# A convolution pair of the in-projection moved from plain column tiles to seven-product form, with the scan and token work around it

## The chip, the cores and the metric

The kernel runs on one core of a Trainium2 chip. The metric is the device time of one execution in microseconds, and the number compared is the median of several executions. Beside it there is one profiled execution, from which all rows of the trace are taken.

## What is computed

The reference is one layer of a decoder trunk on x of 1024 positions by 1024 channels, in float32:

```python
h = rms_norm(x, g_mix[l])
z = jnp.einsum("bsd,de->bse", h, w_in[l]) + b_in[l]
va, ga, xb, gb, sa, sb = jnp.split(z, cuts, axis=-1)      # 1024, 1024, 1536, 1536, 1024, 1024 columns

u = va * jax.nn.sigmoid(ga)
u = causal_depthwise_conv(u, conv_a_w[l], conv_a_b[l])    # width 31
u = jax.nn.silu(layer_norm(u, ln_g[l], ln_b[l]))
y_a = jnp.einsum("bsc,cd->bsd", u, w_a_out[l])

v = causal_depthwise_conv(xb, conv_b_w[l], conv_b_b[l])   # width 4
v = rg_lru(v, w_rg_a[l], b_rg_a[l], w_rg_x[l], b_rg_x[l], lam[l])   # 16 heads of 96, a scan along the positions
y_b = jnp.einsum("bsc,cd->bsd", v * jax.nn.gelu(gb), w_b_out[l])

m = jax.nn.sigmoid(sa) * y_a + jax.nn.sigmoid(sb) * y_b
x = x + jnp.einsum("bsd,de->bse", m, w_o[l])
h = rms_norm(x, g_mlp[l])
f = jnp.square(jax.nn.relu(jnp.einsum("bsd,df->bsf", h, w_1[l])))
x = x + jnp.einsum("bsf,fd->bsd", f, w_2[l])
return rms_norm(x, g_final)
```

The change concerns the first two lines with z, the product that makes u, and the recurrence.

## The kernel before

**Precision.** Every operand of a large product is split into a high and a low part (float32r), and a product takes three passes: high by high, high by low, low by high. The low part of a weight is made in one of two ways. Either ScalarE writes the high part and VectorE subtracts, or, in `split_dma` (line 63), ScalarE writes the negated source into the low tile, an accumulating DMA of the GpSimd queue adds the source to it (line 66), and ScalarE writes the high part.

**The in-projection in two parts.** The 56 column tiles of 128 columns (VA and GA: convolution branch and its gate, 8 each; XB and GB: recurrence and its gate, 12 each; SA and SB: the two output gates, 8 each) are computed in two stages.

The first part (line 827) has one slot for each entry of the list CH, numbered s, up to NC1 - 1. A slot's product is `chunk_mm` (line 734): 24 steps by two halves of the positions, 48 matmuls. Between its two halves and behind them stand the products of the 16 recurrence heads (`head_mm`, line 544, six matmuls for each gate), about one head for a slot from slot 4 on, head 15 at slot 21 with its second product in slot 22. They write a PSUM tile of which there is one buffer ("ps2"), which ScalarE's sigmoid (`head_gate`, line 555) empties. A column tile of XB goes through a convolution of width 4 (`xb_out`); a pair VA, GA makes u (`u_gate`, a sigmoid on ScalarE, line 603; `u_mul` on VectorE, line 609).

The second part (line 1038) takes pairs of column tiles, listed in ZPAIRS, and computes each pair as a two by two block product with seven block products instead of eight (`z_mm`, line 936: 12 matmuls for each, so 84 for a pair). It needs sums and differences of blocks of the weights (`z_sums`, line 766), prepared weights for each product (`z_lhs`, line 781), and differences of blocks of the tokens: `x_load` (line 680, four transfers from the DRAM copy xu into four tiles), `x_sum` (line 686, four subtractions on VectorE), `x_parts` (line 691, splits into high and low). Products 1, 2 and 3 use the token tiles that the first part has; 6, 7, 5 and 4 need the new ones, in this order of first use. The order of the products of all pairs is written out in `zseq` (line 797): (0,1), (1,1), (0,2), (1,2), (0,6), (0,7), (1,7), (0,5), and so on, as (pair, product). At the step n, `z_mm` is issued for zseq[n] and `z_lhs` for zseq[n + 4]; the weights of the first two, (0,1) and (1,1), are prepared in the last slot of the first part (lines 898 to 900), those of the next two just behind it.

**The recurrence.** Tiles come in four groups of three. For the last group (tiles 9 to 11) `scan_exp` (line 569: for each tile an exponential and a tanh on ScalarE) stands in slot 22, `scan_root` (line 580: three square roots) in slot 23, and `scan_tile` (line 591: product, product, scan, and the store to hd, on VectorE and SyncE) in slots 23, 24 and 25. Those of the group before are in slots 20, 21 and 22. Each of the gates of head 15 is brought to its tiles by three transfers on SyncE's queue (line 565).

**The convolution of width 31.** Each of the 8 tiles of u takes 49 VectorE operations (`conv`, line 620). They are the filler: `fill` (line 459) puts them where its plan of VectorE's time has room.

**What sets the order.** ScalarE, VectorE, TensorE, SyncE and GpSimd issue in the order in which the code is written, in this stage on all five. Work for VectorE that is handed to `later` (line 713) is sorted by its due time at the end of each slot or step (`vector_work`, line 717); the order of the others is that of the calls. What is done in which slot around the border stands in two tables: XS (line 818, by slot of the first part) and ZX (line 1036, by step of the second).

**Buffers.** Most tiles of 128 by 1024 come from one pool, tag "T", with 37 buffers (line 36). An instruction that makes a new tile waits on its own queue until a buffer has been given back by the last user of an earlier tile. In use through the border are 14 token tiles (xh, xl), the running sum of the convolutions, gates, decays and v of the scans, u with two working tiles for the convolution under way, and the token differences. The weights of the second part come into another four buffers, tag "p" (`z_load`, line 753), which heads 3, 7, 11 and 15 use as well, two each (line 524).

Of the kernel before, what the change touches and what calls it, by code (L numbers as in the profile page):

```python
# [30 lines left out]
def trunk_kernel(ctx: ExitStack, tc: tile.TileContext, x, xt_in, xt_eo, vecs, w_in, w_a_out, w_b_pl, w_b_sq,  # L31
# [413 lines left out]
    VA, GA, XB, GB, SA, SB = 0, 8, 16, 28, 40, 48  # L445
# [121 lines left out]
    at_, rooted = {}, {}  # L567
# [23 lines left out]
    def scan_tile(t):  # L591
# [4 lines left out]
        nc.vector.tensor_tensor_scan(i, a, i, 0.0, ALU.mult, ALU.add)  # L596
        nc.sync.dma_start(hd[t], i)

    ut = {}
    yd = dp.tile([8, P, S], F32, name="yd")  # L600
    ysum = []
# [100 lines left out]
                      ALU.subtract)  # L702

    CH = [XB, VA, GA, XB + 1, XB + 2, VA + 1, GA + 1, XB + 3, XB + 4, XB + 5, VA + 2, GA + 2]
    CH += [XB + t for t in range(6, 12)] + [c for j in range(3, 7) for c in (VA + j, GA + j)]
    NU = 7
    CH[-2:] = CH[:-3:-1]
    NC1 = len(CH)
    zps = {n: z0[n] for n in range(N0)}
# [3 lines left out]
    def later(ready, cost, f, *a):  # L713

        todo.append((ready, len(todo), cost, f, a))
# [28 lines left out]
                                 start=n == 0, stop=n == 23)  # L744
        at("P", len(halves) * (n1 - n0) * MM)

    ZPAIRS = [GB + 2 * i for i in range(6)] + [VA + 7] + [SA + 2 * i for i in range(4)]
    ZPAIRS += [SB + 2 * i for i in range(4)]
    NZ = len(ZPAIRS)
    zraw, zs, zo, zb = {}, {}, {}, {}  # L750
    zn = [0]

    def z_load(i, kk):

        zraw[i, kk] = raw = qp.tile([P, 2, 4, P], F32, tag="p", name=f"zw{i}_{kk}", bufs=4)
        c = ZPAIRS[i]
        if c < GA:
# [51 lines left out]
    def z_get(n, f):  # L809
# [5 lines left out]
    head_at = {s: n for n, s in enumerate(HS0)}  # L815

    EXP = {head_slot: g for g, head_slot in enumerate(HS0[4 * g + 3] + 1 for g in range(4))}
    XS = {NC1 - 5: ((x_load, 0),), NC1 - 4: ((x_sum, 0),), NC1 - 3: ((x_load, 1), (x_parts, 0, 6)),
          NC1 - 2: ((x_sum, 1), (x_parts, 0, 7, 5)), NC1 - 1: ((x_parts, 0, 4), (x_parts, 1, 6))}
    made = []  # L820
    head_w(0)
    w_load(3)
# [4 lines left out]
    with tc.manual_schedule(engines=ENGINES):  # L827
        for s in range(3, NC1):
# [30 lines left out]
            c = CH[s - 1]  # L859
# [27 lines left out]
            for d in range(5):  # L887
                if s - d in EXP:
# [6 lines left out]
                    t = 3 * g + d - (2 if g < 3 else 1)  # L895
                    if 3 * g <= t < 3 * g + 3:
                        later(rooted[t], 4.8, scan_tile, t)
            if s == NC1 - 1:
                z_get(0, z_lhs)
                z_get(1, z_lhs)  # L900
            for f, *a in XS.get(s, ()):
                f(*a)
# [71 lines left out]
    def z_out(i, m_, hf, src, name):  # L974
        if ZPAIRS[i] < GA:
            z_u(i, ZPAIRS[i] - VA, m_, hf, src)
            return
        ci = ZPAIRS[i] + m_
        bias = bin_c[:, ci:ci + 1]
# [53 lines left out]
        elif p == 4:  # L1033
            z_out(i, 1, 0, zb[i, "u"], "c")

    ZX = {0: ((x_parts, 1, 7),), 2: ((x_parts, 1, 5),), 4: ((x_parts, 1, 4),)}
    H_AT = {2: (0, 0), 5: (1, 1), 3: (0, 1), 4: (1, 0)}
    with tc.manual_schedule(engines=ENGINES):

# [154 lines left out]
        z_get(3, z_lhs)  # L1194
        u_mul(NU - 1, zps[NC1 - 1])
        vector_work(clk["V"])
        z_h(0, 0, 0)
        for n in range(len(zseq) + 2):
# [9 lines left out]
            if n + 3 < len(zseq):  # L1208
                i, p = zseq[n + 3]
# [760 lines left out]
    with tc.manual_schedule(engines={mybir.EngineType.Activation, mybir.EngineType.DVE,  # L1970
                                     mybir.EngineType.PE}):
        for n in range(len(useq)):
# [4 lines left out]
            while ready < min(len(useq), n + look + 1):  # L1977
                i, p = useq[ready]
# [316 lines left out]
```

## Time and profile before

| | |
|---|---|
| median of 3 runs | 1529.34 us (1529.16 to 1529.37) |
| the profiled execution | 1528.49 us, its span 1526.7 us |
| mean granted clock of TensorE | 0.999 |
| first matmul of the first part's slots in the list above (line 743) | 42.4 us |
| first matmul of the second part (line 944) | 338.56 us |
| last convolution operation (line 662) | 583.59 us |

The page gives busy times of the engines, the busy share in 40 slices, the DMA queues, the chain of work that ended last, and the costliest groups. A timeline row has the start, the time, the engine, the line, the operation, output<-input, and in brackets the idle time before it with what ended it. PE is TensorE, DVE is VectorE, ACT is ScalarE, POOL is GpSimd's queue, SP is SyncE's, and SPq is its issuing of a DMA. A window row has, for PE, PEld, DVE, ACT and POOL, the busy time in the stretch, then the granted clock, the DMA share and GB/s.

### The profile page before, as it was taken

To read this page: it belongs to the slowest core of one execution; us is meant where nothing else is said; L and a number is where in the kernel's file an instruction comes from. 1 tells how busy PE (TensorE), PEld (TensorE's weight loads), DVE (VectorE), ACT (ScalarE), POOL (GpSimd) and SP (SyncE) were. 2 spreads that over 40 slices of the span, in tenths; PEclk is the share of its full clock that TensorE was granted. 3 is DMA by queue.
4 is the path that set the end of the run, shared out by engine and by line. 5 is a ranking of instruction groups with operands and counts; after the bars stand their busy time and mean duration, and the time that the engine had idled before them with its cause. 6 is when DMAs were issued, how large, how long until landed. Compare 5 with 4: busy or idle time off the path is not lost.

```text
span 1526.7 us, 18955 instructions
## 1 busy us (share of the span) xinstructions
PE 1517.1 (99%) x6712; PEld 1248.3 (82%) x6712; DVE 1200.7 (79%) x1640; ACT 928.1 (61%) x1299; POOL 190.7 (12%) x228
## 2 busy tenths in 40 slices
PE   9999999999999999999999999999999999999998
PEld 7878887888888888888888888888888888888886
DVE  6999996999999997788769879755555387777777
ACT  6748688576566667645475777554444455545475
POOL 0111011022222222000022322000000000101010
PEclk9999999999999999999999999999999999999999
DMA  8757778698997789964779897333333974776464
GB/s 352 192 135 165 178 179 187 199 262 211 266 254 179 182 207 277 304 216 120 268 197 302 191 213 174 124 127 111 111 111 111 308 264 125 181 206 171 106 124 152
DMA packets 130911, 295.48 MB, mean 194 GB/s; under 512 B 12800, under 2 KB 34944, under 8 KB 130816
## 3 DMA queue, kind: packets, MB, share of 16 engines
q1 hardware_dynamic: 98960, 214.83, 41.5%
q0 software_dynamic: 31568, 78.92, 27.4%
q8 instruction: 52, 0.85, 0.2%
q10 hardware_dynamic: 288, 0.52, 0.1%
q14 instruction: 43, 0.35, 0.1%
HBM read 148.74 MB, written 60.82 MB: 137 GB/s over the span
## 4 chain that ended last, share of the span: by engine, by line
PE 99%; DMA 0%; DVE 0%; ACT 0%; SPq 0%; issue 0%
PE z L743 16%; PE d2b L2015 2%; PE d1b L2015 2%; PE d0b L2015 2%; PE z L273 2%; PE d3b L2015 2%; PE d0e L2015 1%; PE d3e L2015 1%; PE d3a L2015 1%; PE d2e L2015 1%; PE d1e L2015 1%; PE d1a L2015 1%; PE d0a L2015 1%; PE d2a L2015 1%; PE rg L550 1%; PE rg L552 1%
## 5 line engine op out<-in xcount | busy, mean ns | idle before, releaser
L743 PE MATMUL z<-xh,win_h 128*128 128x512 f32 x368 | 115.4, 391 | 0.0
L743 PE MATMUL z<-xl,win_h 128*128 128x512 f32 x368 | 114.9, 390 | 0.0
L655 DVE SCALAR_TENSOR_TENSOR y<-u,vec,y 128x511 f32<-128x511 f32 (+14 forms) x120 | 88.7, 739 | 0.0
L743 PE MATMUL z<-xh,win_l 128*128 128x512 f32 x368 | 87.5, 389 | 0.0
L655 DVE SCALAR_TENSOR_TENSOR yt<-u,vec,yt 128x511 f32<-128x511 f32 (+6 forms) x112 | 82.9, 740 | 0.0
L655 DVE SCALAR_TENSOR_TENSOR y<-yt,csum,y 128x511 f32<-128x511 f32 (+6 forms) x112 | 82.9, 740 | 0.0
L743 PEld LDWEIGHTS z<-xh,win_h 128*128 128x128 f32 x368 | 69.1, 188 | 16.0 <-ACT win_h L67 0.4
L743 PEld LDWEIGHTS z<-xl,win_h 128*128 128x128 f32 x368 | 69.1, 188 | 14.9
L743 PEld LDWEIGHTS z<-xh,win_l 128*128 128x128 f32 x368 | 69.1, 188 | 14.6
L560 ACT ACTIVATE g<-rg,vec 96x1024 f32<-96x1024 f32 x32 | 35.5, 1111 | 72.7 <-PE rg L552 72.7
L1710 ACT ACTIVATE o<-s 128x512 fp32r<-128x512 f32 x56 | 33.8, 624 | 45.2 <-DVE s L1694 26.4
L66 POOL DMA_DIRECT2D zo<-zw x45 | 38.9, 864 | 133.7 <-ACT zo L65 118.4
L501 DVE SCALAR_TENSOR_TENSOR v<-xb,vec,v 128x1023 f32<-128x1023 f32 (+2 forms) x36 | 46.2, 1282 | 4.4 <-ACT v L492 3.5
L66 POOL DMA_DIRECT2D db_10l<-br x4 | 3.5, 868 | 338.3 <-DMA br<-in_w_dram 253.1
L66 POOL DMA_DIRECT2D win_l<-win_raw x23 | 19.8, 861 | 190.6 <-ACT win_l L65 161.9
L65 ACT ACTIVATE zo<-zw 128x512 fp32r<-128x512 f32 x45 | 28.2, 627 | 24.3 <-PE z10f L944 2.1
L1234 DVE TENSOR_TENSOR o<-s,o 128x512 fp32r<-128x512 f32 x56 | 37.3, 684 | 1.5 <-ACT o L1710 1.5
L66 POOL DMA_DIRECT2D zo<-zs x30 | 26.1, 871 | 75.8 <-ACT zo L65 63.8
L67 ACT ACTIVATE zo<-zw 128x512 fp32r<-128x512 f32 x45 | 28.0, 622 | 0.0
L596 DVE TENSOR_TENSOR_SCAN g<-a,g 128x1024 f32<-128x1024 f32 x12 | 27.5, 2292 | 0.4
L66 POOL DMA_DIRECT2D ga<-gsa x8 | 6.9, 866 | 161.2 <-DMA m<-mbd 150.9
L1234 DVE TENSOR_TENSOR o<-w_raw,o 128x512 fp32r<-128x512 f32 x38 | 25.9, 685 | 0.0
(3178 smaller groups left out, 4908.2 us busy)
## 6 DMA issues: line engine op xcount, KB each, us to landing
w_raw<-in_w_dram SPq DMA_DIRECT2D x32, 512.0 KB, 5.5
br<-in_w_dram SPq DMA_DIRECT2D x32, 512.0 KB, 5.6
ar<-fd SPq DMA_DIRECT2D x32, 512.0 KB, 6.9
zw<-in_w_in_dram SPq DMA_DIRECT2D x28, 512.0 KB, 6.9
win_raw<-in_w_in_dram SPq DMA_DIRECT2D x23, 512.0 KB, 4.8
win_l<-win_raw POOLq DMA_DIRECT2D x23, 512.0 KB, 5.1
zo<-zw POOLq DMA_DIRECT2D x45, 256.0 KB, 5.7
gates<-zg SPq DMA_DIRECT2D x32, 256.0 KB, 4.5
```

The source lines that it names most:

```text
L65: nc.scalar.activation(l, src, AF.Copy, scale=-1.0)
L66: nc.gpsimd.dma_start(l, src, accum_op=ALU.add)
L67: nc.scalar.activation(h, src, AF.Copy)
L273: nc.tensor.matmul(z0[i][:, HALVES[hf]], w0[i][w][:, k, :], xpart(a, hf, k), start=k == 0 and which == "hh", stop=k == 7 and which == ("hl ...
L501: nc.vector.scalar_tensor_tensor(v[:, d:S], a[:, 0:S - d], cbw_c[:, w * 12 + t:w * 12 + t + 1], v[:, d:S], ALU.mult, ALU.add)
L560: nc.scalar.activation(a, gps.pop((n, gi))[:HD, :], AF.Sigmoid, bias=(ba_c, bx_c)[gi][:, n:n + 1])
L596: nc.vector.tensor_tensor_scan(i, a, i, 0.0, ALU.mult, ALU.add)
L655: nc.vector.scalar_tensor_tensor(o[:, k:], a[:, 0:HS - k], c, o[:, k:], ALU.mult, add)
L743: nc.tensor.matmul(zps[s][:, HALVES[hf]], w[:, k, :], xw[k][part][hf], start=n == 0, stop=n == 23)
L1234: tt(l, src, h.bitcast(F32), ALU.subtract)
L1710: nc.scalar.activation(o[:, 0], src, AF.Copy)
L2015: nc.tensor.matmul(o, a, b, start=start and n == 0, stop=stop and n == len(todo) - 1, skip_group_check=not start or not stop)
```

## The change

The seventh convolution pair (VA + 6, GA + 6) leaves the list of the first part, which so has 24 entries instead of 26, and enters ZPAIRS as the fifth of 16 pairs. The loop of the first part ends with slot 23. The last two scans move into steps 0 and 3 of the second part. The token work is set anew: in slots counted from the start, `x_load` of the first half comes in slot 20 instead of 21 and of the second half in 22 instead of 23 (one later counted from the loop's end: NC1 - 4 and NC1 - 2); two token parts move into the second part. The rest that is tied to NC1 moves with it: the four `z_load` from slot 23 to 21, the weights of (0,1) and (1,1) from slot 25 to 23. In slot 23 now stand both the roots of the last scan group and those weights.

```diff
+    def scan_later(t):
+        later(rooted[t], 4.8, scan_tile, t)
...
-    CH += [XB + t for t in range(6, 12)] + [c for j in range(3, 7) for c in (VA + j, GA + j)]
-    NU = 7
+    CH += [XB + t for t in range(6, 12)] + [c for j in range(3, 6) for c in (VA + j, GA + j)]
+    NU = 6
...
-    ZPAIRS = [GB + 2 * i for i in range(6)] + [VA + 7] + [SA + 2 * i for i in range(4)]
+    ZPAIRS = [GB + 2 * i for i in range(4)] + [VA + 6] + [GB + 8, GB + 10, VA + 7]
+    ZPAIRS += [SA + 2 * i for i in range(4)]
...
-    XS = {NC1 - 5: ((x_load, 0),), NC1 - 4: ((x_sum, 0),), NC1 - 3: ((x_load, 1), (x_parts, 0, 6)),
-          NC1 - 2: ((x_sum, 1), (x_parts, 0, 7, 5)), NC1 - 1: ((x_parts, 0, 4), (x_parts, 1, 6))}
+    XS = {NC1 - 4: ((x_load, 0),), NC1 - 3: ((x_sum, 0),), NC1 - 2: ((x_load, 1), (x_parts, 0, 6, 7)),
+          NC1 - 1: ((x_sum, 1), (x_parts, 0, 5), (x_parts, 1, 6))}
...
-    ZX = {0: ((x_parts, 1, 7),), 2: ((x_parts, 1, 5),), 4: ((x_parts, 1, 4),)}
+    ZX = {0: ((scan_later, 10), (x_parts, 1, 7)), 1: ((x_parts, 0, 4),), 2: ((x_parts, 1, 5),), 3: ((scan_later, 11),),
+          4: ((x_parts, 1, 4),)}
```

## The prediction

> **What bounds the kernel now.** The page comes first: the engines' busy times and the chain that ended last.
>
> ```profile
> span 1526.7 us, 18955 instructions
> PE 1517.1 (99%) x6712; PEld 1248.3 (82%) x6712; DVE 1200.7 (79%) x1640; ACT 928.1 (61%) x1299; POOL 190.7 (12%) x228
> PE 99%; DMA 0%; DVE 0%; ACT 0%; SPq 0%; issue 0%
> ```
>
> TensorE is busy for 1517.1 of 1526.7 us, and the chain runs on it for 99% of the span. So each matmul that is left out is a gain, and each wait of TensorE is a loss, one for one. The view of waits, for TensorE alone over the whole span, starts with this row, and has only one more, of 1.0 us; both lie ahead of 42 us, before the stage that changes.
>
> ```profile
> PE z L273 <- ACT xh L235: 1.3, 1, 1.3
> ```
>
> So nothing is waiting there that the change could give back. The chain in order of time, then the timeline of TensorE, give the rates and the slots:
>
> ```profile
> 338.73 2.72 PE z0a L944 x12
> ```
>
> ```profile
> 285.31 0.40 PE L550 MATMUL rg<-vth,rgh 96*96 96x512 f32 x1
> ...
> 300.44 0.63 PE L743 MATMUL z<-xh,win_h 128*128 128x512 f32 x2
> ...
> 305.92 0.61 PE L743 MATMUL z<-xh,win_h 128*128 128x512 f32 x2
> ...
> 316.80 0.62 PE L743 MATMUL z<-xh,win_h 128*128 128x512 f32 x2
> ...
> 338.56 0.39 PE L944 MATMUL z0a<-xh,zo 128*128 128x512 f32 x1
> ...
> 339.02 0.61 PE L944 MATMUL z0a<-xh,zo 128*128 128x512 f32 x2
> ```
>
> A product of the second part (12 matmuls) takes 2.72 us. Slot 23 of the first part runs from 305.92 to 316.80, 10.88 us for one column tile. The second part begins at 338.56, and its third matmul, at 339.02, is the first to read the low part of the product's weights. 316.80 is where slot 24 begins; in the changed kernel, whose loop ends with slot 23, the second part stands there.
>
> **The work taken out.** Convolution pair 6 was two column tiles, 2 x 10.88 = 21.76 us, and becomes seven products, 7 x 2.72 = 19.04 us: **-2.72 us** (96 matmuls to 84). This is all that TensorE gains, for nothing else on it changes.
>
> **The last slot of the first part.** ScalarE issues in written order. Its timeline through the same stretch, with the copies that prepare the first product's weights at its end:
>
> ```profile
> 300.64 1.12 ACT L560 ACTIVATE g<-rg,vec 96x1024 f32<-96x1024 f32 x1 [2.84 <-PE rg L552]
> 301.77 1.28 ACT L576 ACT_TABLE_LOAD   x1
> 303.07 1.16 ACT L576 ACTIVATE a<-g,c 128x1024 f32<-128x1024 f32 x1
> ...
> 309.77 1.04 ACT L65 ACTIVATE win_l<-win_raw 128x1024 fp32r<-128x1024 f32 x1
> ...
> 311.79 1.28 ACT L584 ACT_TABLE_LOAD   x1
> 313.08 2.96 ACT L584 ACTIVATE g<-g 128x1024 f32<-128x1024 f32 x3
> ...
> 319.19 1.28 ACT L605 ACT_TABLE_LOAD   x1 [2.20 <-DVE g L596]
> 320.49 1.12 ACT L605 ACTIVATE u<-z,vec 128x1024 f32<-128x1024 f32 x1
> 321.50 1.05 ACT L65 ACTIVATE win_l<-win_raw 128x1024 fp32r<-128x1024 f32 x1
> ...
> 330.71 0.62 ACT L65 ACTIVATE zo<-zw 128x512 fp32r<-128x512 f32 x1
> ```
>
> ```profile
> 331.63 0.86 POOL L66 DMA_DIRECT2D zo<-zw  x1 [3.68 <-ACT zo L65]
> ```
>
> ```profile
> DMA to landing us min/median/max: 3.2/6.7/7.8
> ```
>
> ```profile
> zo<-zw POOLq DMA_DIRECT2D x4, 256.0 KB, 5.4
> ```
>
> Today the copy for product (0,1) starts at 330.71, 7.85 us before TensorE gets there; its accumulating DMA is issued at 331.63 and lands 5.4 us later, at 337.03, against a need at 339.02: 2 us to spare. The roots (313.08) are two slots earlier. In the changed kernel the exponentials stay in slot 22, and slot 23 is both the slot of the roots and the last one, so ScalarE's written order there is: gate of convolution 5, three roots, then the copies for (0,1). The chain starts at 300.64 with the gate of head 15, which waits for TensorE (2.84 us idle before it), so it can't start sooner. Its end follows from the rows: the roots end at 313.08 + 2.96 = 316.04 now; the weight copies of slot 24 go (311.79 - 309.77 = -2.02); two token copies, (x_parts, 0, 6, 7), take their place (2 x 1.0, the pitch from 320.49 to 321.50); the gate with its table load comes ahead of the roots (321.50 - 319.19 = 2.31). That is 318.33. Then 0.92 from copy to issue and 5.4 to landing: 324.65. TensorE needs it at 316.80 + 0.46 = 317.26. So TensorE waits **7.4 us**, 5.2 with the shortest landing of the row and 9.8 with the longest. Nothing hides it, for the matmuls are in written order too. The product after next, (0,2), gets its copies behind those for (0,1) and (1,1) and three token copies, some 5 us later: landed at 324.65 + 5 = 329.7, and TensorE, that late, needs it at 324.65 + 2.26 + 2.72 + 0.46 = 330.1. I cost it at 0; the wait ahead of it is its cover, and 0.4 us is thin.
>
> Of table loads, the Trainium skill (ScalarE: Activation LUTs, What ACT_TABLE_LOAD costs) says 1283 ns and a drain of some 1380 ns more for each switch. The row agrees with the first (1.28) and not with the second: 1.30 us from the load's start at 301.77 the next activation runs. By the page the gate ahead of the roots would make the wait some 1.4 us longer.
>
> **The queue of SyncE.** The four loads of the first products' weights move from slot 23 to slot 21, into four buffers ("p") of which two hold head 15 until its last matmul, just ahead of 300.44. SP issues in order, so behind the third load stand the store of scan 7, the six transfers that complete the gate tiles of head 15, and (x_load, 1).
>
> ```profile
> 294.92 8.63 SPq L565 DMA_DIRECT2D g<-g  x6
> ...
> 307.92 2.24 SPq L761 DMA_DIRECT2D zw<-in_w_in_dram  x4
> ```
>
> ```profile
> g<-g SPq DMA_DIRECT2D x6, 128.0 KB, 2.3
> ```
>
> Today the first gate transfers go out at 294.92; then they go out after 300.44 + 3 x 0.56 (2.24 for four loads) = 302.1, and land some 0.6 + 2.3 us on, at 305.0. The first exponential starts at 303.07 now: **+2 us** on the chain above. It is 0 if the transfers are not held, and up to 5.6 if they also queue behind the two loads just issued (1 MB at 294 GB/s, the rate of a row further down, is 3.6 us).
>
> **The token loads.** (x_load, 0) moves from slot 21 to slot 20. It takes 4 of the 37 buffers "T". I count their tenants at 280 us, when the gate of head 14 asks for one: xh and xl without two 14, ysum 1, scans 7 and 8 with a decay and two gates each 6, gates of tiles 9 and 10 4, v9 to v11 3, two parts of tile 11 2, convolution 3 with u, y, yt 3, and the token loads 4: 37. The gate would be the 38th.
>
> ```profile
> 280.05 1.11 ACT L560 ACTIVATE g<-rg,vec 96x1024 f32<-96x1024 f32 x1 [4.18 <-PE rg L552]
> ```
>
> ```profile
> 274.85 0.68 DVE L646 TENSOR_TENSOR yt<-u 128x512 f32<-128x512 f32 x1
> ...
> 278.01 1.22 DVE L593 SCALAR_TENSOR_TENSOR g<-a,g 128x1024 f32<-128x1024 f32 x1
> ...
> 279.39 1.22 DVE L595 TENSOR_TENSOR g<-g,g 128x1024 f32<-128x1024 f32 x1
> 280.65 2.29 DVE L596 TENSOR_TENSOR_SCAN g<-a,g 128x1024 f32<-128x1024 f32 x1
> ...
> 291.40 5.00 DVE L480 TENSOR_TENSOR xs<-xs,xs 128x1024 f32<-128x1024 f32 x4
> ```
>
> ```profile
> 272.40 0.33 SPq L597 DMA_DIRECT2D hd<-g  x1
> ...
> 278.20 5.09 SPq L684 DMA_DIRECT2D xs<-xu  x4
> ```
>
> ```profile
> hd<-g SPq DMA_DIRECT2D x2, 512.0 KB, 7.0
> ```
>
> Today the loads themselves do the waiting (5.09 us for four issues, to the end of scan 7), on a queue where it costs nothing. One slot earlier they get their buffers first, and ScalarE's gate waits instead, for what scan 7 gives back after its product (279.39 + 1.22). That has moved too, because (x_sum, 0), 5.00 us on VectorE, is now written ahead of scan 7: 285.6. A second delay comes before it: convolution 3, begun at 274.85, needs a buffer that the store of scan 6 gives back 7.0 us after its issue at 272.40, at 279.4; that is 0 to 4.5 us, and I take 2.5. So the gate ends at 285.6 + 2.5 + 1.11 = 289.2. It empties the only PSUM buffer of the heads, into which TensorE's next head product goes at 285.31: a wait of **4 us**, 1.4 without the second delay and 6 with all of it; 0 if the buffers fall otherwise.
>
> **What is hidden.** The rest lies beside matmuls in the second part.
>
> ```profile
> 377.00:396.00 19.00, 19.00 (x86) 15.73 (x85) 17.35 (x28) 11.32 (x21) 5.16 (x7) 1.00 1.06 294
> 586.00:605.00 19.00, 19.00 (x86) 15.73 (x85) 11.48 (x16) 13.53 (x22) 5.15 (x6) 1.00 1.08 304
> ```
>
> ```profile
> L480 DVE TENSOR_TENSOR zo<-zs,zo 128x512 fp32r<-128x512 f32 x30 | 20.7, 689 | 3.9 <-ACT zo L788 3.9
> ```
>
> ```profile
> 583.59 0.69 DVE L662 TENSOR_TENSOR y<-y,yt 128x511 f32<-128x511 f32 x1
> ```
>
> Pair 6 as products adds some 5.6 us to VectorE (ten operations on 512 elements at 0.69, less one of twice that length) and 6 us to ScalarE (twelve copies of weights at 0.62, four of results and two sigmoids, less four copies and a sigmoid of twice the length), plus up to four table loads of 1.28 where its sigmoids stand among gelus. ScalarE is busy 11.32 of 19 us there. VectorE is busy 17.35, but with convolution taps, which give way: their last operation is the one at 583.59, and past that VectorE is at 11.48 of 19. The two scans, 4.9 us each (278.01 to 282.94), that move behind the border take the place of some 15 taps there; the new wait gives them more room. I cost all of it at 0; if the taps did not give way, up to 3 us.
>
> **The sum.** -2.72 + 7.4 + 2 + 4 = +10.7 us. The profiled execution took 1528.49 us (span 1526.7 and 1.8 around it), so 1539.2; the median of the runs is 1529.34, 0.85 above it, and the forecast is 1529.34 + 10.7 = **1540 us**.
>
> **Rivals.** One wait only: the buffers fall otherwise and the gate transfers aren't held, -2.72 + 5.2 to 7.4 = +2.5 to +4.7: 1531.8 to 1534. For it: nothing in the trace shows which instruction is granted a buffer first. Against: the count is one over 37 in either order.
>
> Not slower: the first weights are ready in time and the gain stands alone, 1529.34 - 2.72 = 1526.6. That is decided at one point: the copy for (0,1) must start 0.92 + 5.4 - 0.46 = 5.9 us ahead of the end of slot 23. Against it: by the rows it starts 1.5 us behind it. For it: only that the written order might not be ScalarE's; but at 330.71 it is.
>
> Heavier: the clock falls after the waits. The granted clock is 1.00 in every slice here, but no wait of TensorE in this run is above 1.3 us. If after each of two waits one product ran at half clock, that would cost 2 x 2.72 = 5.4 more: 1545.4. The Trainium skill (TensorE: Matmul & The Clock Gate, Part 1) says that an idle window of about 3.4 us halves the clock until as long a busy one; an estimate by it is 1.7 us for each wait. No run here shows it. In the same case I put a VectorE that falls behind: 3 us more, 1543.
>
> **Chances.** Forecast, both waits with the clock held: 0.63. One wait: 0.13. Not slower: 0.10. Heavier: 0.14. The forecast's bounds are -2.72 + 5.2 + 0 + 1.4 = +3.9 and -2.72 + 9.8 + 5.6 + 6 = +18.7; its ends together are unlikely, so the range is **1531 to 1549**, which holds most of the heavier case and leaves out the case that isn't slower. A measurement tells 0.2%, 3.06 us, from no change. Below 1526.3: half of the third case, 0.05. Up to 1532.4: the other half and part of the second, 0.10. Above: 0.85.
>
> **What would show it.** 6700 matmuls. At slot 21, an idle TensorE before the second head product, with ScalarE's gate waiting on VectorE's L595. On SP, the third weight load held to the end of head 15. At the first product (0,1), TensorE idle some 7 to 9 us, released by the weights' DMA, with the roots right ahead of the copies on ScalarE. The forecast is wrong if TensorE crosses that border without a gap, or if gaps open further into the second part.

## The result, and the profile after

The changed kernel takes **1563.04 us** (median of 4 runs, 1561.58 to 1564.72) against 1529.25 us of the kernel before on the same chip: a ratio of 1.0227, 95% interval 1.0214 to 1.0239, so some 34 us slower. The forecast was 1540 us with a range of 1531 to 1549: the sign was right, the size (10.7 us) less than a third of what came. The profiled execution took 1562.88 us, its span is 1561.1 us, 34.4 us above that of before. Of all executions of the runs below, one of 4200.35 us, in the run with the border written anew, is left out of its median.

Lines of the changed file lie 3 to 4 below those of the old one: L743 is now L746, L944 is L948, L761 is L765, L605 is L608. First two rows of the page of the changed kernel:

```profile
PE 1521.5 (97%) x6700; PEld 1249.9 (80%) x6700; DVE 1205.2 (77%) x1649; ACT 936.4 (60%) x1316; POOL 192.8 (12%) x231
PEclk9999999879999999999999999999999999999999
```

TensorE has 12 matmuls less (6700) and is yet busy for 4.4 us longer, and two slices of the clock row show an 8 and a 7 where all were 9. Both say that some matmuls ran slower. The view of waits for TensorE, which had two rows before, now starts with:

```profile
PE z0a L948 <- ACT zo L67: 12.8, 1, 12.8
PE rg L550 <- ACT g L560: 9.5, 1, 9.5
PE z14f L948 <- DMA zo<-zw: 2.8, 1, 2.8
PE z0a L948 <- DMA zo<-zw: 1.8, 1, 1.8
```

The second row is the wait in slot 21 (9.5 us). The first and fourth are the first product of the second part (14.5). The third is a late wait in the second part; further down stand three more of that kind, at z15e, z3e and z6e (2.8 + 1.2 + 1.0 + 0.8 = 5.8 us in all), and one of 0.2 at z0a. No step of the prediction had these. Then the windows over the first two waits: busy time and number of matmuls, granted clock, DMA share, GB/s.

```profile
286.00:294.00 8.00, 0.00 (x0) 0.61 0.01 3
294.00:298.00 4.00, 3.70 (x9) 0.50 0.32 65
298.00:302.00 4.00, 4.00 (x19) 0.99 0.34 67
...
340.00:344.00 4.00, 1.71 (x3) 0.50 0.62 113
344.00:348.00 4.00, 4.00 (x11) 0.50 1.04 242
348.00:352.00 4.00, 3.85 (x14) 0.84 0.57 169
```

Behind each of the two waits the clock is at 0.50: 9 matmuls from 294 to 298 and 11 from 344 to 348, where 4 us hold 19 at full clock. TensorE's busy time should have been 1517.1 - 2.7 = 1514.4 and is 1521.5, so it grew by **7.1 us**. With this the ledger of the span closes: -2.7 for the matmuls, +9.5, +14.5, +5.8, +0.2 for the waits, +7.1 of busy time, in all +34.4. Most of the 7.1 is the halved clock, and the windows say how much. Behind the first wait it lasts from 294.30 to 298.1, 3.8 us. Behind the second it lasts from 340.53 to 349.3, 7.0 us without the wait of 1.8 in between. At half clock half of such a time is lost: 1.9 + 3.5 = **5.4 us**. The other 1.7 us are not placed one by one; among them is the overlap of neighbouring matmuls (one alone counts 0.39 us, two in a row 0.62), which is lost at each wait.

Now what released the two waits. Here are ScalarE and SyncE's queue, with the gate of head 14 (293.14), the exponentials with their table load (319.66), the roots (336.49) and the copy for product (0,1) (339.35):

```profile
282.23 0.72 ACT L641 ACTIVATE yt<-u,vec 128x512 f32<-128x512 f32 x1 [7.63 <-DMA hd<-g]
293.14 1.11 ACT L560 ACTIVATE g<-rg,vec 96x1024 f32<-96x1024 f32 x1 [10.19 <-DVE g L595]
...
311.43 1.12 ACT L560 ACTIVATE g<-rg,vec 96x1024 f32<-96x1024 f32 x1 [2.84 <-PE rg L552]
319.66 1.28 ACT L576 ACT_TABLE_LOAD   x1 [7.11 <-DMA g<-g]
320.95 1.16 ACT L576 ACTIVATE a<-g,c 128x1024 f32<-128x1024 f32 x1
...
327.65 0.61 ACT L65 ACTIVATE zo<-zw 128x512 fp32r<-128x512 f32 x1
...
331.62 0.61 ACT L65 ACTIVATE zo<-zs 128x512 fp32r<-128x512 f32 x1
...
336.49 2.95 ACT L584 ACTIVATE g<-g 128x1024 f32<-128x1024 f32 x3
339.35 0.61 ACT L65 ACTIVATE zo<-zw 128x512 fp32r<-128x512 f32 x1
```

```profile
267.14 5.46 SPq L687 DMA_DIRECT2D xs<-xu  x4
272.65 0.72 SPq L597 DMA_DIRECT2D hd<-g  x1
...
280.00 32.34 SPq L765 DMA_DIRECT2D zw<-in_w_in_dram  x4
...
312.94 5.06 SPq L565 DMA_DIRECT2D g<-g  x6
```

ScalarE sits idle for 10.19 us ahead of the gate of head 14 until VectorE's L595 gives a buffer back, as forecast. The four weight loads hold SyncE's queue for 32.34 us, to the end of head 15, as forecast; the transfers of the gates go out only at 312.94, and the exponentials wait 7.11 us for them behind a gate that ended at 312.55. The copy for (0,1) stands behind the roots, as forecast.

But ScalarE does not keep to the written order, as the description of the kernel and the prediction say it does. Every copy that writes a zo tile is written behind the roots, and yet six of them ran ahead of the gate and the roots: four from 327.65 and two from 331.62, 3.1 us in all. They are not those that the first product waits for: TensorE starts at 340.53, right behind the copy at 339.87. By what is left to come they belong to (0,2), (1,2) and (0,6), for which the code asks later. What put them there the runs don't show; no step of the prediction has them.

### The profile page after: what moved, and what is told of

Read it like the earlier page. It is cut to its first block, busy times and chain, and to the rows that moved or that the text cites. A ratio compares the mean times of both kernels' runs of the same rounds, so it can differ in the third digit from the quotient of the medians.

```text
span 1561.1 us, 18991 instructions
## 1 busy us (share of the span) xinstructions
PE 1521.5 (97%) x6700; PEld 1249.9 (80%) x6700; DVE 1205.2 (77%) x1649; ACT 936.4 (60%) x1316; POOL 192.8 (12%) x231
## 4 chain that ended last, share of the span: by engine, by line
PE 91%; DMA 4%; issue 2%; DVE 1%; ACT 1%; POOL 0%; SPq 0%; POOLq 0%; ACTq 0%; DVEq 0%
PE z L746 13%; PE z L273 2%; PE d2b L2020 2%; PE d1b L2020 2%; PE d0b L2020 2%; DMA zo<-zs 2%; PE d3b L2020 2%; PE d0e L2020 1%; PE d2e L2020 1%; PE d1a L2020 1%; PE d3e L2020 1%; PE d2a L2020 1%; PE d3a L2020 1%; PE d0a L2020 1%; PE d1e L2020 1%
## 5 line engine op out<-in xcount | busy, mean ns | idle before, releaser
L746 PE MATMUL z<-xh,win_h 128*128 128x512 f32 x336 | 106.1, 393 | 0.0
L746 PE MATMUL z<-xl,win_h 128*128 128x512 f32 x336 | 105.3, 391 | 0.0
L746 PE MATMUL z<-xh,win_l 128*128 128x512 f32 x336 | 79.9, 390 | 0.0
L746 PEld LDWEIGHTS z<-xh,win_h 128*128 128x128 f32 x336 | 63.4, 189 | 14.8 <-ACT win_h L67 0.4
L746 PEld LDWEIGHTS z<-xl,win_h 128*128 128x128 f32 x336 | 63.4, 189 | 13.7
L746 PEld LDWEIGHTS z<-xh,win_l 128*128 128x128 f32 x336 | 63.1, 188 | 13.3
L65 ACT ACTIVATE zo<-zw 128x512 fp32r<-128x512 f32 x48 | 30.0, 626 | 26.2 <-PE z9f L948 2.1
L67 ACT ACTIVATE zo<-zw 128x512 fp32r<-128x512 f32 x48 | 29.8, 621 | 0.0
L550 PE MATMUL rg<-vth,rgh 96*96 96x512 f32 x48 | 19.6, 408 | 9.5 <-ACT g L560 9.5
```

Of the source, the lines that this page charges most:

```text
L65: nc.scalar.activation(l, src, AF.Copy, scale=-1.0)
L67: nc.scalar.activation(h, src, AF.Copy)
L746: nc.tensor.matmul(zps[s][:, HALVES[hf]], w[:, k, :], xw[k][part][hf], start=n == 0, stop=n == 23)
```

## The experiments

Two theories stood against each other. **Border**: everything is lost to buffers, queues and written order around the border between the two parts. **Load**: pair 6 and the late scans are more than VectorE and ScalarE can carry in the second part, and the border only shows it first. Every time is a median, beside the kernel before on the same chip (1528.2 to 1529.0).

### The token loads one slot later

```diff
-    XS = {NC1 - 4: ((x_load, 0),), NC1 - 3: ((x_sum, 0),), NC1 - 2: ((x_load, 1), (x_parts, 0, 6, 7)),
-          NC1 - 1: ((x_sum, 1), (x_parts, 0, 5), (x_parts, 1, 6))}
+    XS = {NC1 - 3: ((x_load, 0),), NC1 - 2: ((x_sum, 0), (x_load, 1)),
+          NC1 - 1: ((x_parts, 0, 6, 7), (x_sum, 1), (x_parts, 0, 5), (x_parts, 1, 6))}
```

> One edit on the changed kernel: the first four token loads and their sums go one slot later (loads in slot 21, sums in slot 22, the copies of tiles 6 and 7 in slot 23), so that the gate of head 14 asks for its buffer before the loads do. Theory (border: buffers and written order): the wait of 9.5 us on the head product in slot 21 goes, and with it some 2 us of halved clock; the wait ahead of the first product (14.5 us) stays: 1563.0 - 11.5 = about 1551.5 us. Rival (the load of pair 6 and of two scans in the second part is too much for VectorE and ScalarE): the border only shows work that is late anyway, and the time stays within 3 us of 1563.

1552.19 us, ratio 1.0154 (1.0139 to 1.0169). The wait on L550 is gone from the view of waits. It is 10.9 us less than the changed kernel: the theory's 11.5, not the rival's 0 to 3.

### One more buffer, no order changed

```diff
+    ex = stage.enter_context(tc.tile_pool(name="extra", bufs=1))
...
-        xq[c2] = {n: T(f"xs{n}_{c2}") for n in (11, 12, 22, 21)}
+        xq[c2] = {n: ex.tile([P, S], F32, name=f"xs{n}_{c2}") if c2 == 0 and n in (12,) else T(f"xs{n}_{c2}")
+                  for n in (11, 12, 22, 21)}
```

> One edit on the changed kernel, no order changed: one of the four early token tiles (xs12 of the first pair) lies in a buffer of its own beside the 37 of the pool, which so has one free when the gate of head 14 asks. Theory (the gate is the 38th tenant): the wait of 9.5 us in slot 21 goes although the token loads stay one slot early, and with it the halved clock behind it: about 1551.5 us, as with the loads a slot later. If the gate were short of more than one buffer the wait stays, at 5 us or more, and the time above 1556. Rival (the loads cost by their traffic or by the sums on VectorE, not by a buffer): the wait stays at 9.5.

1549.05 us, ratio 1.0135 (1.0120 to 1.0150). The loads come as early as in the changed kernel, the sums on VectorE too, and yet the wait in slot 21 is gone; the view of waits of this run starts at the border.

```profile
PE z0a L950 <- ACT zo L67: 12.1, 1, 12.1
```

So the gate was short of exactly one buffer: the count of 37 tenants in the prediction was right, and 14.0 us hung on it. That is 2.7 more than the wait and its clock cost in the next run. The view of waits has most of this: the late waits at z14f, z3e, z6e and z15e, 5.8 us in the changed kernel, are 2.2 + 0.7 + 0.4 = 3.3 us here.

### The same part alone, on the kernel before

```diff
-    XS = {NC1 - 5: ((x_load, 0),), NC1 - 4: ((x_sum, 0),), NC1 - 3: ((x_load, 1), (x_parts, 0, 6)),
+    XS = {NC1 - 6: ((x_load, 0),), NC1 - 5: ((x_sum, 0),), NC1 - 3: ((x_load, 1), (x_parts, 0, 6)),
```

> One part of the change alone, on the kernel before: the first four token loads go from slot 21 to slot 20, their sums from 22 to 21. All else, the 26 slots and seven pairs too, as before. Theory: the wait in slot 21 comes with it, 9.5 us and some 2 us of halved clock, for nothing in it hangs on the pair that is removed; the two slots behind it hide nothing of it, since TensorE itself waits: 1529 + 11.5 = about 1540.5 us. By the prediction's own size (4 us): 1533. Rival (it needs the shorter first part): 1529.

1539.48 us, ratio 1.0072 (1.0056 to 1.0089): 11.3 us more than before, as the theory had it. Nothing of the pair's move is needed for this loss.

### The clock by itself

```diff
                 head_gate(before, 0, begun)
+                if before == 14:
+                    for _ in range(36):
+                        nc.tensor.matmul(zps[s][:, HALVES[0]], zero, xw[0][0][0], start=False, stop=False)
```

> The clock by itself, on the kernel before with the four early token loads (one wait of 9.1 us in slot 21, 1539.5 us): 36 matmuls with zero weights are added ahead of the head product that waits, which add zero to the tile in progress; at 0.227 us each they fill 8.2 us of the wait. Theory (the clock halves because TensorE idles): the clock stays at 1.00 through slot 21, the wait shrinks to about 1 us, and the kernel with 36 matmuls more is faster by the 2 us that the halved clock costs: about 1537.4 us. Rival (the clock falls with the memory traffic or something else at that time, or the loss of some 2 us lies elsewhere): the same time within 1 us, 1538.5 to 1540.5.

1538.06 us, ratio 1.0069 (1.0057 to 1.0082), against 1539.48. The 1.4 us between them decide nothing: 1538.06 lies between the theory's 1537.4 and the rival's 1538.5, and the executions overlap (1537.93 to 1541.10 with the added matmuls, 1538.83 to 1540.31 without). The profiles decide. TensorE is busy for 1526.2 us against 1520.2, 6.0 us more, where 36 matmuls at 0.227 are 8.2: the others take 2.2 us less. Windows of the run without the added matmuls, then of the run with them:

```profile
288.00:290.00 2.00, 0.00 (x0) 0.70 0.00 0
...
294.00:298.00 4.00, 3.75 (x9) 0.50 0.48 163
```

```profile
288.00:290.00 2.00, 2.00 (x10) 1.00 0.00 0
...
294.00:298.00 4.00, 3.68 (x16) 1.00 0.45 156
```

The DMA share is 0.00 in both from 284 to 294 us, so traffic is not what lowers the clock; the idle time of TensorE is. In the first run the clock falls 3.6 us after TensorE went idle at 285.2 (the window 288 to 290 has it at 0.70, so it falls at 288.8) and is still at 0.50 when work has begun again.

### The weight loads one slot later

```diff
-            if s == NC1 - 3:
+            if s == NC1 - 2:
                 for i in range(4):
                     z_load(i // 2, i % 2)
```

> One edit on the changed kernel: the four loads of the first products' weights go from the end of slot 21 to the end of slot 22, so SyncE's queue is not held by them while head 15 still has two of their buffers. Theory: the transfers that complete the gates go out as their gates end; the exponentials, which waited 7.1 us for them behind the gate, start at once; the wait ahead of the first product falls from 14.5 us to 7 or 8, and the wait in slot 21 stays at 9.5: about 1556 us. If the queue cost only the 2 us that the prediction took: 1561. Rival (load): no change.

1556.06 us, ratio 1.0182 (1.0165 to 1.0199), 7.0 us less than the changed kernel, as the theory had it. The exponentials now run straight behind the gate, and the first product waits 5.1 us for the copy and 2.2 for the DMA, 7.3 in all. The copies run in the written order in this run.

### The same part alone, on the kernel before

```diff
-            if s == NC1 - 3:
+            if s == NC1 - 5:
                 for i in range(4):
```

> One part of the change alone, on the kernel before: the four loads of the first products' weights go from the end of slot 23 to the end of slot 21, where the third must wait for head 15's buffers. Theory: the transfers of the gates go out late here too, and the exponentials of slot 22 start 6 or 7 us later, but two more slots (21.8 us) lie between them and the first product, so TensorE waits for nothing: 1529, within 2 us. Rival (the held queue costs by itself, for instance through the weights of slot 24, which stand behind it): 1532 or more.

1535.67 us, ratio 1.0048 (1.0033 to 1.0062): 7.5 us more than before, and the theory (nothing, two slots of cover) was wrong; the rival's 1532 or more holds. The two slots did not cover what comes next on ScalarE:

```profile
283.30 18.05 SPq L761 DMA_DIRECT2D zw<-in_w_in_dram  x4
```

```profile
310.51 1.28 ACT L576 ACT_TABLE_LOAD   x1 [8.79 <-DMA g<-g]
...
319.44 1.04 ACT L67 ACTIVATE win_h<-win_raw 128x1024 fp32r<-128x1024 f32 x1
```

```profile
320.53 0.73 PE L743 MATMUL z<-xh,win_h 128*128 128x512 f32 x2 [3.61 <-ACT win_h L67]
...
321.57 1.00 PE L743 MATMUL z<-xh,win_h 128*128 128x512 f32 x2
```

Late transfers make the exponentials late (8.79 us behind the gate), and in ScalarE's order the copies of slot 24's weights stand behind the exponentials. TensorE waits 3.61 us for them, and 1 us after it has begun again, two matmuls take 1.00 us in place of 0.62. So 3.6 us of wait, 0.7 of small waits, and 2.9 by which TensorE's busy time grew (1520.0 us, with the same 6712 matmuls) make the 7.2 us by which the span is longer. SyncE's held queue was paid here, too, at the next thing that ScalarE prepared for TensorE.

### Both undone

This is the changed kernel with the token loads and the weight loads each one slot later, the two diffs above together.

> Two edits together on the changed kernel: the early token loads a slot later and the four weight loads at the end of slot 22. It leaves the one term of the prediction that has not been tested by itself, the copies for (0,1) behind the gate and the roots on ScalarE, which it put at 7.4 us. Theory: the two terms taken out add up (11 and 7 us less than 1563), so about 1545 us: the wait in slot 21 gone, the first product waiting 7 to 8 us with some 2 us of halved clock behind it, and 5 us of late waits. If the prediction's 7.4 us were the whole of what is left: 1534. Rival (what is freed is eaten by the following products): 1550 or more.

1546.41 us, ratio 1.0119 (1.0104 to 1.0134). This is 16.6 us less than the changed kernel, where the two by themselves gave 10.9 and 7.0: they add up, to within 1.3 us. The largest wait that is left is the first term of the prediction:

```profile
311.18 1.12 ACT L608 ACTIVATE u<-z,vec 128x1024 f32<-128x1024 f32 x1
...
313.61 2.96 ACT L584 ACTIVATE g<-g 128x1024 f32<-128x1024 f32 x3
316.47 0.61 ACT L65 ACTIVATE zo<-zw 128x512 fp32r<-128x512 f32 x1
```

```profile
317.65 0.50 PE L948 MATMUL z0a<-xh,zo 128*128 128x512 f32 x1 [0.67 <-ACT zo L67]
...
324.83 1.22 PE L948 MATMUL z0a<-xh,zo 128*128 128x512 f32 x2 [6.44 <-DMA zo<-zw]
```

ScalarE goes through gate, roots and copy in the order that the prediction wrote down, and TensorE gets the low part of the first weights at 324.83. The prediction's working had 324.65. The wait is 0.67 + 6.44 = 7.1 us, where it said 7.4. Two errors of 2 us cancel in this: the copy starts at 316.47, not 318.33, since the token copies stand behind it here, and the DMA takes 7.4 us from its issue, not 5.4.

### The first copies ahead of the roots

```diff
             w_load(s + 2)
+            if s == NC1 - 1:
+                z_get(0, z_lhs)
+                z_get(1, z_lhs)
```

> One edit on the changed kernel: the copies for the first two products (0,1) and (1,1) are written at the head of slot 23, ahead of the gate of convolution 5 and of the three roots. Theory: the copies start behind the last tanh, some 11 us earlier; what is left of the wait of 14.5 us is the way through the accumulating DMA (6 us) less nothing: 5 to 6 us, so about 1553 to 1555. The roots and the token copies go behind them, and the products from the third on may be late for that by up to 4 us, which would leave 1557 to 1559. Rival (load): the wait only moves to the following products, no change within 3 us.

1562.44 us, ratio 1.0220 (1.0205 to 1.0235): nothing gained, where 8 to 10 us were expected, or 4 to 6 with the later products late. The time is the rival's (within 3 us of 1563), and so is what happened: the wait moved to the products behind. The first product waits 5.7 + 1.9 us instead of 14.5, but two rows have come in:

```profile
PE z0a L948 <- ACT z0b L1014: 4.0, 1, 4.0
PE z1a L948 <- ACT z1b L1014: 1.5, 1, 1.5
```

TensorE's third and fourth products, (0,2) and (1,2), add to the banks of the first and second, and ScalarE must have copied these (z0b from z0a, z1b from z1a) before. The copies stand behind the roots and token copies, so what the first product no longer waits, the third does. The prediction had not listed this: it had looked at the third product's weights only. And the first product's copies start at 332.49, 4.0 us behind the last tanh and not right behind it, since two token copies and again four copies for later products ran ahead of them.

### All three edits, and the border written anew

The three edits together (token loads, weight loads, first copies):

> The three edits together on the changed kernel. Theory: no wait in slot 21, the exponentials early, the first product's weights in time; what the change gains (2.7 us) then shows, less what the later products wait: the copies for (1,2) now stand behind the roots and four token copies, which by the rows (2.3 + 4.2 + 5 us of ScalarE behind 313) puts their landing some 6 us behind TensorE. So 1533 to 1538 us with that wait, and 1527 to 1532 without it. Rival (load): the waits come back further into the second part, and the time stays above 1550.

1553.84 us, ratio 1.0165 (1.0150 to 1.0180): worse than the first two without the third (1546.41), and above 1550, where the rival had it, though by waits at the border and not further on. The weight loads stand behind the second token loads, which wait for buffers on SyncE's queue, and the bank copy behind a token copy that waits for one:

```profile
316.05 0.63 ACT L65 ACTIVATE zo<-zw 128x512 fp32r<-128x512 f32 x1 [6.30 <-DMA zw<-in_w_in_dram]
...
339.84 1.06 ACT L703 ACTIVATE xs7h<-xs 128x1024 fp32r<-128x1024 f32 x1 [5.62 <-DVE g L595]
```

Neither was in the expectation. So the order was written out with these two in mind; the buffer of its own for one token tile and the first copies at the head of slot 23 are in this run too:

```diff
+    XS = {NC1 - 3: ((x_load, 0), (z_load, 0, 0), (z_load, 0, 1)),
+          NC1 - 2: ((z_load, 1, 0), (z_load, 1, 1), (x_sum, 0), (x_load, 1)),
+          NC1 - 1: ((x_parts, 0, 6, 7), (x_sum, 1))}
...
         z_get(2, z_lhs)
         z_get(3, z_lhs)
+        z_get(4, z_lhs)
+        x_parts(1, 6)
+        scan_root(3)
...
+    ZX = {0: ((x_parts, 1, 7), (scan_later, 9), (scan_later, 10)), 1: ((x_parts, 0, 5),), 2: ((x_parts, 1, 5),), 3: ((scan_later, 11),),
+          4: ((x_parts, 0, 4),), 5: ((x_parts, 1, 4),)}
```

> The border written anew on the changed kernel, with pair 6 among the products as there. The first token loads back in slot 21, with one tile in an own buffer; the weights of (0,*) loaded at the end of slot 21, into the two free buffers, those of (1,*) in slot 22 ahead of the second token loads; copies for (0,1) and (1,1) at the head of slot 23; behind the gate of convolution 5 the copies for (0,2), (1,2) and (0,6), and only then the roots; scans 9 to 11 in the second part. Theory (everything lost was lost to order and buffers at the border): no wait above 3 us there, the matmuls saved show, and with the late waits of the second part (some 5 us) the time is 1527 to 1533 us. Rival (VectorE and ScalarE cannot carry pair 6 and three scans in the second part): waits of over 8 us in all remain past the border, above 1537.

1543.16 us, ratio 1.0098 (1.0081 to 1.0114): 10 us above the theory's range, on the rival's side. The first product's wait is down to 0.83 us; the bank copies, behind the roots, cost 2.5 and 3.8. With the roots moved behind the first bank copy:

```diff
-        scan_root(3)
...
+    ZX = {1: ((scan_root, 3), (scan_later, 9)), 2: ((x_parts, 1, 7),), 3: ((x_parts, 0, 5), (scan_later, 10)), 4: ((x_parts, 1, 5),),
+          5: ((x_parts, 0, 4), (scan_later, 11)), 6: ((x_parts, 1, 4),)}
```

> The run before it (the border written anew) with three things moved: the roots of scans 9 to 11 go behind the copy of z0a into its second bank, which TensorE's third product waits for; the copies of tile 7 of the second pair and of tile 5 stand behind the copy of z1a; scans 10 and 11 stand two products later each. Theory: the waits of 2.5 and 3.8 us on these two copies go, and with them the halved clock; left are 0.8 us at the first product, about 1 us at z1a, some 3 us of late waits: 1528 to 1534 us. The point at which it could fail: with three scans behind the border the copies of tile 5 find no buffer before 331 us, and the eighth product waits 2 to 5 us for their accumulating DMA, with halved clock 1536 to 1540. Rival (VectorE and ScalarE cannot carry it): as the run before, 1543 or more.

1543.26 us, ratio 1.0096 (1.0080 to 1.0111): the same, 9 us above the theory's range and again the rival's time. The waits on the bank copies have shrunk to 0.6 us in all, and others have taken their place. Three of the largest name VectorE: 2.1 us (xs7l) and 1.5 (zc) at z0f, 1.2 (zo) at z0e. The waits at z3e, z6e and z2a, 1.2 to 1.3 us each, name a weights' DMA. The rival begins to hold for the border.

### The late waits

In the changed kernel the chain of work that ended last, in order of time, shows what z3e waited for:

```profile
420.67 0.45 POOL ysum L671
...
422.68 10.19 DMA zo<-zs
```

A weights' DMA is issued at 422.68, behind the one that adds a finished convolution to the running sum (ysum), and lands 10.19 us later; the median of its group (zo<-zs) is 6.6 us. Ahead of the waits at z6e and z14f the DMA of the sum stands likewise (479.08 and 629.20); the wait at z15e has none ahead of it. The next run has the border of the last one and moves that DMA of the sum:

```diff
-            nc.gpsimd.dma_start(ysum[0], acc, accum_op=add)
+            yq.append(acc)
...
+            if n + 4 >= len(zseq) or zseq[n + 4][1] == 3:
+                y_flush()
```

> The run before it (1543.3 us), with one thing more: in the second part the DMA that adds a finished convolution to the sum is issued by GpSimd behind the weights' DMA of a product 3 and ahead of a stretch without one, not at the moment when the convolution ends, so it never stands right ahead of weights that are needed next. Theory (the late waits at z3e and z6e, 2.5 us in that run, are weights that land 10 us after their issue, behind such a DMA of 512 KB): they go, 1540 to 1541 us. Rival (the second part is late there because VectorE and ScalarE carry too much): they stay or move, within 1 us of 1543.3.

1539.56 us, ratio 1.0070 (1.0058 to 1.0083): 3.7 us less, as the theory had it, and the waits at z3e, z6e and z14f are gone; the one at z15e is still there with 1.0. Windows of this run over the second part:

```profile
380.00:450.00 70.00, 70.00 (x311) 1.00 0.86 217
450.00:550.00 100.00, 100.00 (x443) 1.00 0.79 199
```

From 380 to 550 us TensorE is never idle, with pair 6 in it: the second part itself carries the pair. What remains lies before 380 us (TensorE is busy for 56.69 of the 64 us from 316) and behind 550.

### VectorE behind the border

```diff
         a, r, i = at_.pop(t), gate.pop((0, t)), gate.pop((1, t))
+        full = i
+        if t > 8:
+            a, r, i = a[:, 0:16], r[:, 0:16], i[:, 0:16]
...
-        nc.sync.dma_start(hd[t], i)
+        nc.sync.dma_start(hd[t], full)
```

> The run with the sums in the gap (1539.6 us), with the arithmetic of scans 9 to 11 cut to the first 16 of 1024 positions (the stores stay whole), so that VectorE is given back about 14 us behind the border; what these scans compute is left out. Rival to the theory, now in part adopted (VectorE cannot carry three scans beside the first twelve products): the waits of TensorE released by VectorE (xs7l 2.1, zc 1.5, zo 1.2, xs5l 0.3 us) fall to under 1.5 us together and the halved clock of some 3 us goes: 1532 to 1536 us. Theory in its pure form (only order, buffers and the latency of the DMAs): the same waits stay, 1538.5 to 1540.5.

This kernel leaves out what scans 9 to 11 compute past their first 16 positions, so it is no version to use; it gives VectorE 12.6 us back (1193.4 us busy against 1206.0). 1536.30 us, ratio 1.0049 (1.0035 to 1.0062), is 3.3 us less: just above what the rival gave, and far from the theory's pure form. All four waits that named VectorE are gone (5.1 us), and three that name a DMA have come in their stead (2.2 + 1.6 + 0.6). Windows of the run before it and of this one, with all engines (busy time of PE, PEld, DVE, ACT, POOL; clock; DMA share):

```profile
332.00:340.00 8.00, 5.87 (x19) 4.43 (x18) 7.83 (x10) 5.46 (x8) 1.72 (x2) 0.79 0.76 197
```

```profile
332.00:340.00 8.00, 8.00 (x37) 6.64 (x36) 5.52 (x15) 7.88 (x12) 2.97 (x4) 1.00 1.04 276
340.00:352.00 12.00, 7.67 (x29) 5.22 (x29) 4.32 (x6) 7.68 (x14) 2.61 (x3) 0.97 1.08 283
```

With the scans, VectorE is busy 7.83 of the 8 us from 332 to 340, TensorE 5.87. Without them VectorE falls to 5.52 and TensorE has no gap there, but the DMA share is then 1.04 and 1.08 and the larger gaps, from 347 us on, wait for transfers. So behind the border VectorE's time for the scans is one limit, and by these rows the transfers of token parts, gates, weights and stores, which all fall into the same 20 us, are another one close to it.

## Why the prediction was wrong

Its direction was right, and so were its three mechanisms, their places and their order, though ScalarE kept the written order, on which it built, only in part. It failed in the sizes of two terms, and in two things that it priced at nothing. Of the 23.7 us by which the span exceeds the sum of +10.7, the token loads are 5.5, SyncE's queue is 5.1, the late waits with the small one at z0a are 6.0, and TensorE's longer busy time is 7.1.

**The token loads (said 4 us, measured 9.5).** This term was mis-sized in its second delay: "that is 0 to 4.5 us, and I take 2.5". The working tile of convolution 3 had to wait for the store of scan 6. The prediction let that store land 7.0 us after its issue, by the median; in the changed kernel it was issued at 272.65, right behind the four token loads (267.14), and what waited for it ran at 282.23, 9.6 us later. The prediction's row for VectorE's first operation of that convolution had 274.85; now it stands here:

```profile
282.30 0.69 DVE L649 TENSOR_TENSOR yt<-u 128x512 f32<-128x512 f32 x1 [8.02 <-DMA hd<-g]
...
291.82 1.22 DVE L595 TENSOR_TENSOR g<-g,g 128x1024 f32<-128x1024 f32 x1
```

That is 7.4 us late, not 2.5, and beyond the bound of 4.5 too. The second row is the product that gives the buffer back, at 291.82 instead of 279.39: 12.4 us, 5.0 for the sums and 7.4 for the store. A landing time taken from a stretch without the loads did not hold for a store right behind them; that it was the loads that slowed it is read from the queue's order and was not tried by itself.

**SyncE's queue (said 2 us, measured 7.1).** The prediction named the case that came, "up to 5.6 if they also queue behind the two loads just issued", and took 2 as the value. The transfers went out when it said: 312.94 lies 1.5 us behind the start of head 15's last gate (311.43), as 302.1 lies behind 300.64. But from issue to landing it used 2.3 us, the median of before, and the row of 312 to 322 us has:

```profile
g<-g SPq DMA_DIRECT2D x6, 128.0 KB, 6.1
```

The exponentials' table load starts at 319.66, 6.7 us behind the first issue, where the prediction had 2.9: 3.8 us more. And this table load waited for the transfer as well, where the prediction let it run ahead: 1.3 us more, which its bound of 5.6 does not have. The run with the weight loads one slot later gave 7.0 us back.

**The first product's weights (said 7.4, measured 7.3 and 7.1).** The wait, its place and its cause were forecast, by following ScalarE instruction by instruction through rows that existed. That the size agrees to 0.3 us is luck. With both loads later, the copy starts 1.9 us earlier than worked out, and its DMA takes 2.0 us longer. With the weight loads alone later, the gate waits 2.56 us for VectorE, so the copy starts 2.6 us later than worked out, and the DMA takes 3.7 us in place of 5.4. In the changed kernel itself the six copies that ran ahead put the copy 3.1 us back, and the DMA takes 3.2.

**The clock (said 0 in the forecast, 5.4 in the rival at 0.14; measured 5.4, of 7.1 us more busy time).** The prediction wrote that no run here shows it and so gave it a small chance. The rule from the Trainium skill (TensorE: Matmul & The Clock Gate, Part 1), that an idle window of about 3.4 us halves the clock until as long a busy one, is borne out where the wait is long: in the run with the early loads on the kernel before, the fall comes 3.6 us into the idle time. The prediction's estimate by this rule, 1.7 us for each wait, is close to what was lost in slot 21, 1.9 us. Behind the second wait, which was two with 1.2 us of work between them, 3.5 us were lost. The rival's 5.4 was right to the tenth, though not by its working (one product at half clock behind each wait), and it should have stood in the sum.

**The second part (said 0 to 3 us, measured 5.8 in late waits, and 7.3 of waits in the first twelve products when the border was mended).** "I cost all of it at 0". The cover named there, convolution taps that give way, exists; but the late waits at z3e, z6e and z14f, 4.6 of the 5.8, came from a finished convolution whose sum's DMA was issued right ahead of a weights' DMA, and they went when that DMA was moved. The one at z15e, 1.2, stays unexplained. And once the border waits are taken out, VectorE's three scans do show: "the new wait gives them more room" was true only as long as the wait was there. In that run (1539.56 us) TensorE's busy time is 4.3 us above 1514.4 as well; the clock of 0.97 from 316 to 380 us accounts for 1.9 of them.

The cover of 0.4 us that the prediction called thin, for (0,2), wasn't tested by weights, which were copied early, but by the bank copy, which the prediction had not followed at all.

On table loads the trace again agrees with the Trainium skill (ScalarE: Activation LUTs, What ACT_TABLE_LOAD costs) on the load, 1.28 us at 319.66, and not on the drain: the next exponential starts at 320.95, 1.29 us after the load's start.

No version tried here is faster than the kernel before. The 12 matmuls less are there in each of them, but the pair's two slots were also the time in which the last scans gave their buffers back and the second part's first weights, banks and token parts were made; the best border with all work in it is still 0.7% slower. Whether some other order gains is open. That the DMA share above 1 is what stops the last run was read, not tried.

## What to carry to other kernels

Where ScalarE's order decides, look at the order that it kept in the trace, and count on copies of later work to come between. When work is taken out of a stretch whose engine is always busy, ask first what that stretch was covering on the other engines, and list everything that must be ready at its new end: weights, banks, parts and buffers, each with its queue. An instruction moved earlier takes its buffer earlier: count the pool's tenants, and where the count is one over, price the wait to the release that ends it, with landing times from rows that have the same traffic. Most waits of TensorE of 2 us or more cost some 2 us of halved clock on top here (1.9 behind the one of 9.5 us, 1.7 behind the one of 3.61), and this should stand in the sum with them.

## What the runs showed of the hardware

The granted clock follows TensorE's idle time with a lag: in the run with the weight loads early on the kernel before, it fell only 1 us after a wait of 3.61 us had already ended, and matmuls took half as long again or more until 325 us, so part of a wait's cost lies behind it.

How long a wait must be is not settled by its length alone. Two rows of the same place late in the second part, z14f, each with the window behind it, first of the run with the weight loads one slot later, then of the changed kernel:

```profile
633.89 1.22 PE L948 MATMUL z14f<-xs4h,zo 128*128 128x512 f32 x2 [2.06 <-DMA zo<-zw]
634.00:636.00 2.00, 2.00 (x5) 0.50 1.09 317
```

```profile
641.20 0.73 PE L948 MATMUL z14f<-xs4h,zo 128*128 128x512 f32 x2 [2.83 <-DMA zo<-zw]
642.00:644.00 2.00, 2.00 (x10) 1.00 1.09 283
```

The wait of 2.06 us halved the clock, a shorter one than the 3.4 us that the prediction cites from the Trainium skill (TensorE: Matmul & The Clock Gate, Part 1), and the longer one of 2.83 us left it at 1.00. What else decides is open.

Matmuls that add zero, put into a wait, kept the clock at 1.00 through it. The time of the kernel with them, 1538.06 against 1539.48 us, is not clearly different.

A DMA's landing time depended on when it was issued: for the same 256 KB of weights it was 3.2 us behind the roots of the changed kernel, 5.4 in the median of four in the kernel before, 7.4 in the run with both loads later, and 10.2 right behind an accumulating DMA of 512 KB. The last of these is the one that was tried: with that DMA moved, its waits were gone.
